# Attention row sums added up whole on two engines, and a side lane with pinned places

## The chip, the cores and the metric

The kernel runs on one core of a Trainium2 chip. The core has five instruction queues that run side by side and wait for each other through semaphores: PE (TensorE, the matrix engine; its weight loads are listed as PEld), DVE (VectorE), ACT (ScalarE), POOL (GpSimd) and SP (SyncE, which here only issues DMAs). Each queue runs its instructions strictly in the order in which the program lists them. The metric is the device time of one execution in microseconds (us), lower is better. Three runs of the kernel before gave 2798.85, 2803.77 and 2807.2 us.

## What is computed

One layer of a streaming encoder for two groups of requests: a prompt of 2048 frames and a sample group of 8 streams with 16 new frames each and 1024 cached ones. Cut to what matters here:

```python
u, q, k, v, logf = _mixer_inputs(x, ...)          # one projection, two groups of heads
# group A: depthwise conv of width 31, LayerNorm over 512 channels, swish
y32 = (y32 - mu) * lax.rsqrt(var + EPS) * ln_g + ln_b
# group B: attention, 8 heads of 64, causal, with a forget bias
s = einsum('bqhd,bkhd->bhqk', q, k) * HEAD_DIM ** -0.5
s = s + (cum_q[..., :, None] - cum_k[..., None, :])
p = softmax(where(mask, s, NEG_INF))
attn = einsum('bhqk,bkhd->bqhd', p, v)
x = x + g1 * (concat([conv_out, attn]) @ w_out)   # output projection
x = x + g2 * ((silu(h @ w_gate) * (h @ w_up)) @ w_down)
```

The softmax needs, for each query, the sum of the exponentials over all keys; it is computed with the keys on the 128 partitions, so a sum over keys is a sum over partitions and over key tiles.

## The kernel before

The program has these stages in time: input projections (to about 575 us), the prompt's attention (to about 1178 us), the output projection, and the feed-forward part (from about 1290 us to the end).

**Attention.** `attention` runs 16 *steps*, one for each pair of heads `p` (4) and block `qb` of 512 queries (4). A step goes over `4 * qb + 4` key tiles `kt` of 128 keys. For each key tile and each of the two heads, `attend` issues two matmuls into a bank `s` (L1004, L1010), a third with the mask on the diagonal (L1012), and one exponential on ACT into a tile `e` (L1014). Such a head and key tile is called a *unit* below; there are 320. Two key tiles later `values` multiplies `e` with V into `pv` (L971), both heads side by side in the array. Tiles with `kt < 4 * qb` lie below the diagonal and are 512 queries wide; the four others are 512, 384, 256 and 128 wide.

**Sums.** Below the diagonal POOL adds the exponentials of two neighbouring key tiles, for each head, into `two` (L980); PE multiplies each `two` with a matrix of ones into the bank `sm` (`add_up`, L960). Four such matmuls fit side by side in the array: a matmul with a group number `g` writes 32 rows of `sm` from row 32 g on. Diagonal tiles go into `sm` without an addition.

**Maxima.** `score_maxima` runs some 30 to 50 units ahead: it multiplies the same queries and keys once more (`mx`, L923, two banks) and DVE reduces each product to a maximum (`M`, L928). PE's second next `mx` waits for its bank, so for that reduction.

**End of a step.** ACT copies `pv` to `zc` (L991; `zc` has two buffers, so step n+2 takes that of step n) and `sm` to SBUF; the sums go through DRAM to another layout (`load`), are inverted on DVE (`invert`, L1058), come back spread over partitions (`back`), and DVE multiplies `zc` by them (`divide`, L1066), after which SP stores `zc` to `cat_d` (L1067). These four are due 2, 6, 9 and 14 units after the end of the step.

**The lane.** `background` is work with no place of its own in the attention: the conv's LayerNorm for five chunks (`conv_norm`), then the whole attention of the sample group (`sample_setup`, eight times `sample_batch`). It has one PSUM bank (`lane`), so each of its matmuls waits for the reader of the one before. A batch is a chain: keys times queries for two halves of the cache and the new frames (L1074), each added to `S` on DVE (L1175), maximum (L1181), exponential on ACT (L1182), transposes (L1189, L1195) with copies on ACT, probabilities times V (L1207), scaling (L1211), a transpose (L1214) and two copies into `catS` (L1217). Each `yield` in it is a point between which the weaving of the generators sets attention work.

**Order.** A list scheduler decides the order on each queue from priorities (the lane's are 1000 lower, `BACK_BY`) and its own estimate of when operands are there. `after` forbids an instruction to be set ahead of a named one on the same engine, without a wait. The wrapper `behind` did this for some of the lane's matmuls.

The output projection (`project_out`) takes all eight PSUM banks as accumulators `acc` (L1244), that of the lane for the last of the eight column blocks.

Of the kernel before, what the change touches and what calls it, by code (L numbers as in the profile page):

```python
# [118 lines left out]
class Layer:  # L119
# [587 lines left out]
    def conv_norm(self, ch, sp, bank):  # L707
# [9 lines left out]
        def channel_mean(src):  # L717
            pm = bank
            for j in range(4):
                self.behind(nc.tensor.matmul)(pm[32 * j:32 * j + 32, :n], self.ones[:, 0:32], src[j], start=True, stop=True,  # L720
                                 tile_position=(0, 32 * j))
            m = sp.tile([P, 512], F32, tag="cm", name="cm")
            nc.scalar.copy(m[:, :n], pm[:, :n])
            po = bank
            nc.tensor.matmul(po[:, :n], self.mean, m[:, :n], start=True, stop=True)
            return po

        mu = channel_mean([y[:, j, :n] for j in range(4)])
        ms = sp.tile([P, 512], F32, tag="cw", name="cmu")
        nc.scalar.copy(ms[:, :n], mu[:, :n])  # L730
        yield
        sqs = []
        for j in range(4):
            nc.vector.tensor_tensor(y[:, j, :n], y[:, j, :n], ms[:, :n], ALU.subtract)
            sq = sp.tile([P, 512], F32, tag="cq", name="cq", bufs=4)
            nc.scalar.activation(sq[:, :n], y[:, j, :n], AF.Square)
            sqs.append(sq[:, :n])
        yield
        var = channel_mean(sqs)
        v = sp.tile([P, 512], F32, tag="cv", name="cvar")[:, :n]  # L740
        nc.vector.tensor_scalar(v, var[:, :n], EPS, None, ALU.add)
        r = sp.tile([P, 512], F32, tag="cr", name="cr")[:, :n]
        nc.scalar.activation(r, v, AF.Ln)
        nc.scalar.activation(r, r, AF.Exp, scale=-0.5)
        newton_rsqrt(nc, r, sp.tile([P, 512], F32, tag="cm", name="ct")[:, :n], v, 1)
        yield
        for j in range(4):
            z = y[:, j, :n]
            nc.vector.tensor_tensor(z, z, r, ALU.mult)
# [30 lines left out]
    def attention(self, ctx):  # L780
# [4 lines left out]
        self.waiting, self.due, self.last_s = [], [], None  # L785
# [11 lines left out]
        nback, done, units, scored = 15 + 5 * 9 + 12 + 8 * 11, 0, 0, AHEAD  # L797
# [147 lines left out]
    def attend(self, p, qb, n):  # L945
# [5 lines left out]
        z, sums = [], []  # L951

        started = set()

        def add_up(terms, last=False):
            if terms and not started:
                z.append(self.bank("tr", "sm"))
# [7 lines left out]
        def values(kt, off, es):  # L965
# [10 lines left out]
            if kt < 4 * qb:  # L976
                if kt % 2 == 0:
                    for h in range(2):
                        two = wk.tile([P, 512], F32, tag="two", name="two", bufs=6)
                        nc.gpsimd.tensor_tensor(two, es[h], self.waiting[0][3][h], ALU.add)  # L980
                        sums.append((2 * (kt // 2 % 2) + h, 0, two))
                elif kt % 4 == 1:
                    ready, sums[:] = sums[:-2], sums[-2:]
                    add_up(ready)
                return
            sums.extend((2 * (kt % 2 if qb else 0) + h, off, es[h]) for h in range(2))
            if kt % 2 == 0:
                return
            if kt == nkt - 1:
                zc = wk.tile([P, 512], F32, tag="zc", name="zc")  # L990
                self.last_exp = nc.scalar.copy(zc, z[0])  # L991
            add_up(sums, kt == nkt - 1)
            sums.clear()
            if kt == nkt - 1:
                self.end_of_step(p, qb, zc, z[1])

        for kt in range(nkt):
# [4 lines left out]
            for h in range(2):  # L1002
# [10 lines left out]
                e = wk.tile([P, 512], F32, tag="e", name="e", bufs=12)  # L1013
# [17 lines left out]
    def end_of_step(self, p, qb, zc, sums):  # L1031
# [37 lines left out]
        self.due += [(self.nscore + k, f) for k, f in ((2, load), (6, invert), (9, back), (14, divide))]  # L1069

    def behind(self, op):

        def issue(*args, **kw):
            ins = op(*args, **kw)  # L1074
            self.after(ins, self.last_s)
            return ins
        return issue

    def sample_setup(self, bank):
# [27 lines left out]
        for kt in range(8):  # L1107
            self.behind(nc.tensor.matmul)(pt[:n, 2 * kt:2 * kt + 2], lf[:, kt, :], self.ones[:, 0:2], start=True, stop=True)
        suf = sm.tile([P, 8], F32, name="suf")
        nc.vector.memset(suf[:n, 7:8], 0.0)  # L1110
        for kt in range(6, -1, -1):
            nc.vector.tensor_tensor(suf[:n, kt:kt + 1], pt[:n, 2 * kt + 2:2 * kt + 3], suf[:n, kt + 1:kt + 2], ALU.add)
        yield
        for b in range(2):
            pb = bank.rearrange("p (i k) -> p i k", i=4)
            for i in range(4):
                self.behind(nc.tensor.matmul)(pb[:n, i, :], lf[:, 4 * b + i, :], tri, start=True, stop=True)
            nc.vector.tensor_tensor(
                bias[:n, b * 512:(b + 1) * 512].rearrange("p (i k) -> p i k", i=4), pb[:n],
# [7 lines left out]
        nc.tensor.matmul(pn[:n, :], lm.rearrange("p s h -> p (s h)"), sel[:, NS:], start=True, stop=True)  # L1127
# [25 lines left out]
    def sample_batch(self, b, bank):  # L1153
# [4 lines left out]
        for c in range(3):  # L1158
# [8 lines left out]
            pc = bank  # L1167
            for g in range(NP):
                self.behind(nc.tensor.matmul)(pc[32 * g:32 * g + 32, :w], self.Qbd[:, g, b].rearrange("p h q -> p (h q)"), kt[:, g, :],
                                              start=True, stop=True, tile_position=(0, 32 * g))  # L1170
# [4 lines left out]
            nc.vector.tensor_tensor(S[:, c0:c0 + w], S[:, c0:c0 + w], pc[:, :w], ALU.add)  # L1175
            if c == 2:
                nc.vector.tensor_tensor(S[:, c0:], S[:, c0:], self.maskS, ALU.add)
            yield
        nm = sm.tile([P, 1], F32, tag="nm", name="nm", bufs=2)
        rs = sm.tile([P, 1], F32, tag="rsx", name="rsx", bufs=2)  # L1180
        nc.vector.tensor_reduce(nm, S, AX.X, ALU.max, negate=True)  # L1181
        nc.scalar.activation(S, S, AF.Exp, bias=nm, accum_out=rs)  # L1182
        nc.vector.reciprocal(rs, rs)
# [582 lines left out]
```

## Time and profile before

| | before |
|---|---|
| median of 3 runs | 2803.77 us |
| the profiled execution | 2804.06 us, of which 2802.3 us are the span of its instructions |
| PE busy | 2719.9 us, 97% |
| DVE busy | 1975.1 us, 70% |
| ACT busy | 1237.1 us, 44% |
| POOL busy | 461.2 us, 16% |
| mean granted TensorE clock | 0.985 |

Busy shares are of the whole span. PE is a pipeline whose ends are modelled, so a busy PE can still wait a little inside a matmul. In a row of the groups, "x96 | 127.2, 1342 | 398.3 <-ACT e" reads: 96 instructions, 127.2 us busy (overlaps counted once), 1342 ns for one, and 398.3 us in which the engine sat idle before them, mostly for that ACT instruction. A row of the timeline begins with its start and length in us; an idle time ahead of it, if any, stands in brackets at its end with what ended it. An fp32 matmul counts as two instructions there.

### The profile page before, as it was taken

To read this page: it belongs to the slowest core of one execution; us is meant where nothing else is said; L and a number is where in the kernel's file an instruction comes from. 1 tells how busy PE (TensorE), PEld (TensorE's weight loads), DVE (VectorE), ACT (ScalarE), POOL (GpSimd) and SP (SyncE) were. 2 spreads that over 40 slices of the span, in tenths; PEclk is the share of its full clock that TensorE was granted. 3 is DMA by queue.
4 is the path that set the end of the run, shared out by engine and by line. 5 is a ranking of instruction groups with operands and counts; after the bars stand their busy time and mean duration, and the time that the engine had idled before them with its cause. 6 is when DMAs were issued, how large, how long until landed. Compare 5 with 4: busy or idle time off the path is not lost. (4 is left out here: it accounts for less than half of the span.)

```text
span 2802.3 us, 48143 instructions
## 1 busy us (share of the span) xinstructions
PE 2719.9 (97%) x16666; PEld 2388.6 (85%) x16666; DVE 1975.1 (70%) x3951; ACT 1237.1 (44%) x2406; POOL 461.2 (16%) x616
## 2 busy tenths in 40 slices
PE   7999999999999999999999999999999999999999
PEld 6899988864445545499999999999999999999999
DVE  2798898966465454235397989877886778766765
ACT  4443323344343444434354446444554446555552
POOL 3454411222222222214201121000000000000000
PEclk9999999989999999999999999999999999999999
DMA  9753567674426676355576869866786769788873
GB/s 328 248 192 107 189 220 265 203 199 123 124 73 192 175 233 176 116 192 187 177 265 205 305 204 314 272 217 214 240 288 208 227 194 319 245 279 262 274 252 116
DMA packets 406348, 603.49 MB, mean 215 GB/s; under 512 B 61556, under 2 KB 264468, under 8 KB 404056
## 3 DMA queue, kind: packets, MB, share of 16 engines
q1 hardware_dynamic: 405976, 600.31, 66.7%
q8 instruction: 131, 2.15, 0.3%
q14 instruction: 113, 0.93, 0.1%
q0 software_dynamic: 128, 0.11, 0.0%
HBM read 426.00 MB, written 174.25 MB: 214 GB/s over the span
## 5 line engine op out<-in xcount | busy, mean ns | idle before, releaser
L1556 PE MATMUL z<-rT,rW 128*128 128x360 f32 (+1 forms) x8316 | 1383.7, 328 | 4.5 <-ACT rW L1260 1.4
L1556 PEld LDWEIGHTS z<-rT,rW 128*128 128x128 f32 x8316 | 1379.8, 188 | 6.3 <-ACT rW L1260 2.1
L1260 ACT ACTIVATE rW<-rR 128x512 fp32r<-128x512 f32 x714 | 434.1, 616 | 382.5 <-PE z L1556 275.9
L1261 DVE TENSOR_TENSOR rW<-rR,rW 128x512 fp32r<-128x512 f32 x714 | 476.8, 673 | 149.3 <-ACT rW L1260 144.7
L702 DVE SCALAR_TENSOR_TENSOR cv<-cu,cpar,cv 128x384 f32<-128x384 f32 x580 | 311.7, 615 | 2.9 <-ACT cv L700 2.9
L928 DVE TENSOR_REDUCE M<-mx 128x1 f32<-128x512 f32 (+2 forms) x320 | 189.7, 607 | 146.5 <-PE mx L923 105.2
L1014 ACT ACTIVATE e<-s 128x512 f32<-128x512 f32 (+3 forms) x320 | 168.4, 533 | 278.2 <-PE s L1012 140.2
L514 PE MATMUL z<-hqx,wqh 128*128 128x384 f32 (+1 forms) x768 | 197.5, 333 | 0.1
L980 POOL TENSOR_TENSOR two<-e 128x512 f32<-128x512 f32 x96 | 127.2, 1342 | 398.3 <-ACT e L1014 328.0
L1260 ACT ACTIVATE rT<-traw 128x360 fp32r<-128x360 f32 (+1 forms) x315 | 149.3, 501 | 91.7 <-DMA traw<-gt_d 58.1
L1261 DVE TENSOR_TENSOR rT<-traw,rT 128x360 fp32r<-128x360 f32 (+1 forms) x315 | 157.7, 531 | 42.7 <-ACT rT L1260 42.4
L923 PEld LDWEIGHTS mx<-K,Q 96*128 96x128 f32 x320 | 63.7, 201 | 116.6 <-DVE M L928 54.7
L923 PE MATMUL mx<-K,Q 96*128 96x512 f32 (+2 forms) x320 | 145.2, 463 | 17.1 <-DVE M L928 12.6
L971 PE MATMUL pv<-e,V 128*64 128x512 f32 (+3 forms) x640 | 156.6, 565 | 3.0 <-ACT zc L991 3.0
L514 PEld LDWEIGHTS z<-hqx,wqh 128*128 128x128 f32 x768 | 136.0, 188 | 16.6 <-issue 12.4
L1484 DVE TENSOR_TENSOR rR<-rR 128x512 f32<-128x512 f32 (+1 forms) x136 | 94.2, 712 | 57.2 <-DMA rR<-w_down 52.0
L1244 PE MATMUL acc<-ch,woh 128*128 128x360 f32 (+1 forms) x384 | 128.1, 336 | 4.9 <-DVE xo L1252 2.6
L1244 PE MATMUL acc<-ch,wol 128*128 128x360 f32 (+1 forms) x384 | 128.1, 334 | 0.0
L1004 PE MATMUL s<-Q,K 128*128 128x512 f32 (+3 forms) x320 | 127.6, 399 | 0.0
L514 PE MATMUL z<-hqx,wql 128*128 128x384 f32 (+1 forms) x384 | 126.5, 329 | 0.0
L1244 PE MATMUL acc<-cl,woh 128*128 128x360 f32 (+1 forms) x384 | 122.3, 331 | 0.0
L1010 PE MATMUL s<-Q,K 128*128 128x512 f32 (+3 forms) x320 | 119.3, 373 | 0.0
(307 smaller groups left out, 3581.5 us busy)
## 6 DMA issues: line engine op xcount, KB each, us to landing
rR<-sup_d SPq DMA_DIRECT2D x176, 256.0 KB
rR<-w_gate SPq DMA_DIRECT2D x132, 256.0 KB
traw<-gt_d SPq DMA_DIRECT2D x154, 180.0 KB
rR<-w_down SPq DMA_DIRECT2D x104, 256.0 KB
rR<-sdn_d SPq DMA_DIRECT2D x96, 256.0 KB
rR<-w_up SPq DMA_DIRECT2D x88, 256.0 KB
sup_d<-rR SPq DMA_DIRECT2D x88, 256.0 KB
wa<-w_ada SPq DMA_DIRECT2D x16, 1024.0 KB
```

The costliest lines, as they stand in the source:

```text
L514: nc.tensor.matmul(z[:, :n], w[:, m], x[:, :n], start=(c == 0 and k == 0), stop=(c == CB - 1 and k == 2))
L702: self.pin(nc.vector.scalar_tensor_tensor(dst, src, w, acc[i], ALU.mult, ALU.add))
L923: self.mx.append(nc.tensor.matmul(mx[:, :w], Q2[0:AUX, h, j * P:(j + 1) * P], K2[kb][0:AUX, h, :w], start=True, stop=not diag))
L928: self.last_max = nc.vector.tensor_reduce(M[:, i, kb:kb + 1], mx[:, :w], AX.X, ALU.max)
L971: product = nc.tensor.matmul(z[0][HD * h:HD * h + HD, off:], V[kt // 4][:, kt % 4, HD * h:HD * h + HD], es[h][:, off:], start=(kt == 0), s ...
L980: nc.gpsimd.tensor_tensor(two, es[h], self.waiting[0][3][h], ALU.add)
L1004: first = nc.tensor.matmul(s[:, off:], K1[kb][:, h, sl], Q1[:, h, off:], start=True, stop=False)
L1014: self.last_piece = nc.scalar.activation(e[:, off:], s[:, off:], AF.Exp)
L1244: self.nc.tensor.matmul(z[:, :n], w[:, m], y, start=(first and i == 0 and k == 0), stop=(last and i == len(terms) - 1 and k == 2))
L1260: copy = self.nc.scalar.activation(hi, raw, AF.Copy)
L1261: engine.tensor_tensor(lo, raw, f32(hi), ALU.subtract)
L1556: nc.tensor.matmul(z, W[:, x, m], t[:, y, :w], start=(k == 0 and i == 0), stop=(k == n - 1 and i == 2))
```

## The change

It has five parts.

1. Below the diagonal the exponentials of a whole step are added up, key tile by key tile, into one tile for each head: head 0's on POOL, head 1's on DVE. PE multiplies the two with the ones once for each step. The groups of the diagonal tiles change so that the first diagonal tile goes beside the two sums; the three others follow at the step's end. `two` goes, `sums` (4 buffers) comes, and `e` has 14 buffers for 12.
2. In `conv_norm` the subtraction of the mean and the product with the reciprocal deviation, each for four tiles, go from DVE to POOL.
3. All lane operations on PE, ACT, DVE and POOL are issued through one wrapper `late`, which keeps each behind the latest attention instruction of its own engine (last `s`, last exponential, last maximum, last addition). The first DVE additions of `attend` use it too.
4. The lane has more yields; the count by which they are spread over the attention is 237 in place of 160.
5. The four pieces of work at a step's end are due 3, 8, 13 and 20 units after it, in place of 2, 6, 9 and 14.

```diff
         def channel_mean(src):
-            pm = bank
             for j in range(4):
-                self.behind(nc.tensor.matmul)(pm[32 * j:32 * j + 32, :n], self.ones[:, 0:32], src[j], start=True, stop=True,
-                                 tile_position=(0, 32 * j))
+                self.pe(bank[32 * j:32 * j + 32, :n], self.ones[:, 0:32], src[j], start=True, stop=True, tile_position=(0, 32 * j))
+            yield
             m = sp.tile([P, 512], F32, tag="cm", name="cm")
-            nc.scalar.copy(m[:, :n], pm[:, :n])
+            self.copy(m[:, :n], bank[:, :n])
+            yield
...
         for j in range(4):
-            nc.vector.tensor_tensor(y[:, j, :n], y[:, j, :n], ms[:, :n], ALU.subtract)
+            self.gp(y[:, j, :n], y[:, j, :n], ms[:, :n], ALU.subtract)
+        yield
+        for j in range(4):
             sq = sp.tile([P, 512], F32, tag="cq", name="cq", bufs=4)
-            nc.scalar.activation(sq[:, :n], y[:, j, :n], AF.Square)
+            self.act(sq[:, :n], y[:, j, :n], AF.Square)
             sqs.append(sq[:, :n])
-        yield
+            yield
...
         for j in range(4):
             z = y[:, j, :n]
-            nc.vector.tensor_tensor(z, z, r, ALU.mult)
+            self.gp(z, z, r, ALU.mult)
...
-        nback, done, units, scored = 15 + 5 * 9 + 12 + 8 * 11, 0, 0, AHEAD
+        nback, done, units, scored = 232 + 5, 0, 0, AHEAD
...
             self.last_product = product
-            if kt < 4 * qb:
-                if kt % 2 == 0:
-                    for h in range(2):
-                        two = wk.tile([P, 512], F32, tag="two", name="two", bufs=6)
-                        nc.gpsimd.tensor_tensor(two, es[h], self.waiting[0][3][h], ALU.add)
-                        sums.append((2 * (kt // 2 % 2) + h, 0, two))
-                elif kt % 4 == 1:
-                    ready, sums[:] = sums[:-2], sums[-2:]
-                    add_up(ready)
+            d = kt - 4 * qb
+            if d < 0:
+                if kt == 0:
+                    held.extend(es)
+                elif kt == 1:
+                    acc.extend(wk.tile([P, 512], F32, tag="acc", name="sums", bufs=4) for h in range(2))
+                if kt:
+                    self.last_add = nc.gpsimd.tensor_tensor(acc[0], es[0], acc[0] if kt > 1 else held[0], ALU.add)
+                    self.late(nc.vector.tensor_tensor, self.last_max)(acc[1], es[1], acc[1] if kt > 1 else held[1], ALU.add)
                 return
-            sums.extend((2 * (kt % 2 if qb else 0) + h, off, es[h]) for h in range(2))
-            if kt % 2 == 0:
-                return
-            if kt == nkt - 1:
+            if d == 0:
+                held[:] = [(h, 0, x) for h, x in enumerate(acc)]
+            part = 2 * (d % 3 == 0 if qb else 0)
+            held.extend((part + h, off, es[h]) for h in range(2))
+            if d == 3:
                 zc = wk.tile([P, 512], F32, tag="zc", name="zc")
                 self.last_exp = nc.scalar.copy(zc, z[0])
-            add_up(sums, kt == nkt - 1)
-            sums.clear()
-            if kt == nkt - 1:
+                add_up(held, True)
                 self.end_of_step(p, qb, zc, z[1])
+            elif d == 1:
+                n = 4 if qb else 2
+                add_up(held[:n])
+                del held[:n]
...
-                e = wk.tile([P, 512], F32, tag="e", name="e", bufs=12)
+                e = wk.tile([P, 512], F32, tag="e", name="e", bufs=14)
...
-        self.due += [(self.nscore + k, f) for k, f in ((2, load), (6, invert), (9, back), (14, divide))]
+        self.due += [(self.nscore + k, f) for k, f in ((3, load), (8, invert), (13, back), (20, divide))]
-    def behind(self, op):
+    def late(self, op, last):
 
         def issue(*args, **kw):
             ins = op(*args, **kw)
-            self.after(ins, self.last_s)
+            self.after(ins, last)
             return ins
         return issue
+    def pe(self, *args, **kw):
+        return self.late(self.nc.tensor.matmul, self.last_s)(*args, **kw)
+    def gp(self, *args):
+        return self.late(self.nc.gpsimd.tensor_tensor, self.last_add)(*args)
```

`flip` (transposes), `act`, `copy` and `dve` are wrappers of the same kind. In `sample_setup` and `sample_batch` every operation with a partner on another engine goes through them, with a yield ahead of most of those that wait.

The scheduler decides the order on each queue anew. Three places.

**PE, from the last attention matmul to the output projection.** `R` is the last one, with which the last step's sums are spread; `lane<-kc` are the key products of a sample batch, `lane<-ident,S` its transposes, `lane<-vc` and `lane<-vn` its products with V, `lane<-ident,ob` its last transpose. Before, the lane rows from `R` on, up to the first matmul `acc`, and then those that follow, the first of them behind 14 `acc`, the others behind 63:

```order
L1043 MATMUL R<-sm,four 128x512
L1074 MATMUL lane<-kc,Qbd 32x512 x4
L1074 MATMUL lane<-kS,Qbd 32x16 x4
L1189 MATMUL lane<-ident,S 128x128 x4
```

```order
L1189 MATMUL lane<-ident,S 128x128 x4
L1195 MATMUL lane<-ident,S 16x128
L1207 MATMUL lane<-vc,pT 32x128 x32
L1207 MATMUL lane<-vn,pTn 32x128 x4
L1214 MATMUL lane<-ident,ob 128x128
```

That is one batch, the eighth, and its first key products already stand ahead of `R`. In the changed kernel the rows around `R`, and then those behind the 63 matmuls `acc`, are these (L1086 is the line of the wrapper `late`):

```order
L1055 MATMUL R<-sm,four 128x512
L1086 MATMUL lane<-ident,ob 128x128
L1086 MATMUL lane<-kc,Qbd 32x512 x8
L1086 MATMUL lane<-kS,Qbd 32x16 x4
```

```order
L1086 MATMUL lane<-ident,S 128x128 x8
L1086 MATMUL lane<-ident,S 16x128
L1086 MATMUL lane<-vc,pT 32x128 x32
L1086 MATMUL lane<-vn,pTn 32x128 x4
L1086 MATMUL lane<-ident,ob 128x128
L1086 MATMUL lane<-kc,Qbd 32x512 x8
L1086 MATMUL lane<-kS,Qbd 32x16 x4
L1086 MATMUL lane<-ident,S 128x128 x8
L1086 MATMUL lane<-ident,S 16x128
L1086 MATMUL lane<-vc,pT 32x128 x32
L1086 MATMUL lane<-vn,pTn 32x128 x4
L1086 MATMUL lane<-ident,ob 128x128
```

The fence ends with the seventh batch; the eighth follows in the same rows, with nothing between, and then the other `acc`. The last transpose of the fifth batch, the sixth, the seventh and the eighth batch now stand behind the last attention matmul. Counted by the units ahead of them on PE, the lane starts its first batch at unit 195 in place of 156 of 320, and the conv's LayerNorm ends at 170 in place of 135.

**DVE, around the division of step (1, 3).** `M` are the maxima, `zc` the division. Before:

```order
L928 TENSOR_REDUCE M_1_6655<-mx_10280 128x1
L1066 TENSOR_TENSOR zc_10030<-zc_10030,aR_10038 128x512
L1058 RECIPROCAL inv_10204<-inv_10204 128x8
L928 TENSOR_REDUCE M_1_6655<-mx_10309 128x1
```

and now:

```order
L938 TENSOR_REDUCE M_1_6655<-mx_9981 128x1
L1078 TENSOR_TENSOR zc_9612<-zc_9612,aR_9622 128x512
L1070 RECIPROCAL inv_9780<-inv_9780 128x8
L1086 TENSOR_TENSOR bias_9242<-lane_7504,suf_9323 64x512
L938 TENSOR_REDUCE M_1_6655<-mx_10022 128x1
```

The division moved from unit 182 to unit 187 (by the maxima ahead of it), and that of steps (0, 3) and (2, 3) alike, from 103 to 107 and from 262 to 267. ACT's copy into the same buffer two steps later, for steps (1, 1), (2, 1) and (3, 1), stands behind 108, 188 and 268 exponentials before, and behind 110, 190 and 270 now. SP's store of `zc` stands between the two in both.

**DVE, in a step below the diagonal,** here (2, 3). `sums` is the new addition for head 1:

```order
L938 TENSOR_REDUCE M_0_6654<-mx_10774 128x1
L1086 RECIPROCAL rsx_9858<-rsx_9858 128x1
L938 TENSOR_REDUCE M_0_6654<-mx_10789 128x1
L1086 TENSOR_TENSOR sums_10639<-e_10724,sums_10639 128x512
L938 TENSOR_REDUCE M_0_6654<-mx_10803 128x1
L938 TENSOR_REDUCE M_0_6654<-mx_10813 128x1
L1086 TENSOR_TENSOR sums_10639<-e_10768,sums_10639 128x512
```

There are 84 such additions on DVE and 84 for head 0 on POOL, in place of 96 on POOL; the matmuls with the ones below the diagonal fall from 96 to 24.

More of the change, by code (lines that the diff above doesn't have):

```diff
@@ L717, in channel_mean @@
         def channel_mean(src):
-            pm = bank
             for j in range(4):
-                self.behind(nc.tensor.matmul)(pm[32 * j:32 * j + 32, :n], self.ones[:, 0:32], src[j], start=True, stop=True,
-                                 tile_position=(0, 32 * j))
+                self.pe(bank[32 * j:32 * j + 32, :n], self.ones[:, 0:32], src[j], start=True, stop=True, tile_position=(0, 32 * j))
+            yield
             m = sp.tile([P, 512], F32, tag="cm", name="cm")
-            nc.scalar.copy(m[:, :n], pm[:, :n])
[L724 to L728, printed above, removed]
+            self.copy(m[:, :n], bank[:, :n])
+            yield
+            self.pe(bank[:, :n], self.mean, m[:, :n], start=True, stop=True)
+            yield
+        yield from channel_mean([y[:, j, :n] for j in range(4)])
         ms = sp.tile([P, 512], F32, tag="cw", name="cmu")
-        nc.scalar.copy(ms[:, :n], mu[:, :n])
+        self.copy(ms[:, :n], bank[:, :n])
         yield
@@ L950, in attend @@
         nkt = 4 * qb + 4
-        z, sums = [], []
-        started = set()
+        z, held, acc, started = [], [], [], set()
         def add_up(terms, last=False):
-            if terms and not started:
+            if not started:
                 z.append(self.bank("tr", "sm"))
@@ L1107, in sample_setup @@
         for kt in range(8):
-            self.behind(nc.tensor.matmul)(pt[:n, 2 * kt:2 * kt + 2], lf[:, kt, :], self.ones[:, 0:2], start=True, stop=True)
+            self.pe(pt[:n, 2 * kt:2 * kt + 2], lf[:, kt, :], self.ones[:, 0:2], start=True, stop=True)
+        yield
         suf = sm.tile([P, 8], F32, name="suf")
@@ L1188, in sample_batch @@
             for i in range(4):
-                nc.tensor.transpose(pp[:, i, :], S[:, (4 * c + i) * P:(4 * c + i + 1) * P], self.ident)
+                self.flip(pp[:, i, :], S[:, (4 * c + i) * P:(4 * c + i + 1) * P], self.ident)
+            yield
             pT = sm.tile([P, 4, P], F32, tag="pT", name="pT", bufs=2)
-            nc.scalar.copy(pT, pp)
+            self.copy(pT, pp)
             pts.append(pT)
-            yield
+        yield
         pp = bank[:, :P]
-        nc.tensor.transpose(pp[:QS, :], S[:, PAST:], self.ident)
+        self.flip(pp[:QS, :], S[:, PAST:], self.ident)
+        yield
         pn = sm.tile([P, P], F32, tag="pTn", name="pTn")
-        nc.scalar.copy(pn[:QS, :], pp[:QS, :])
-        vn = sm.tile([QS, DC], F32, tag="vn", name="vn")
-        nc.sync.dma_start(vn, a["o_v"][T + b * QS:T + (b + 1) * QS, :])
+        self.copy(pn[:QS, :], pp[:QS, :])
         yield
```

72 lines of the change are left out of this document (46 added, 26 removed).

## Prediction

> **What bounds the kernel now.** I read the page's first part, then the busy time by stretches, then the groups and waits of the attention, the only stage whose code changes.
>
> ```profile
> span 2802.3 us, 48143 instructions
> PE 2719.9 (97%) x16666; PEld 2388.6 (85%) x16666; DVE 1975.1 (70%) x3951; ACT 1237.1 (44%) x2406; POOL 461.2 (16%) x616
> 630.00:1177.00 547.00, 526.32 (x3122) 262.50 (x3123) 271.88 (x501) 224.18 (x438) 131.77 (x102) 0.98 0.52 152
> 1177.00:1205.00 28.00, 19.23 (x169) 15.60 (x163) 14.71 (x22) 15.20 (x24) 0.00 (x0) 0.88 0.41 132
> ```
>
> The last two rows are stretches: length, then busy time and count of PE, PEld, DVE, ACT and POOL, then granted clock, DMA share and GB/s. PE is busy for 526 of 547 us of attention, VectorE for half of it. So PE's queue sets the stage: whatever takes PE time or makes PE wait counts in full, and work that moves between other engines counts only where PE waits for it. The second row is the seam to the output projection, where PE is busy for 19 of 28 us, at a clock of 0.88. All later stages keep their code and their PE work, so a delay at the seam reaches the end undiminished. I sum against the profiled execution, 2804.06 us (span 2802.3 and 1.76 around it); the median of the runs, 2803.77, is 0.3 lower, which I neglect.
>
> **1. Fewer matmuls for the sums: -14 us.**
>
> ```profile
> 630.00:1178.00 548.00, 59.10 (x448) 12.53 (x448) 0.98 0.51 151
> L960 PE MATMUL sm<-two,ones 128*32 128x512 f32 x192 | 26.4, 624 | 0.0
> 1172.62 1.06 PE L960 MATMUL sm<-two,ones 128*32 128x512 f32 x8
> 1173.50 1.03 PE L960 MATMUL sm<-e,ones 128*32 128x512 f32 x8
> 1174.46 0.65 PE L971 MATMUL pv<-e,V 128*64 128x256 f32 x4
> ```
>
> The first row is the stretch with line 960 alone: 59 us of PE for all sums. The 192 instructions on `two` are 96 matmuls at 26.4 / 96 = 0.275 us; 72 go, 19.8 us. The starts of the last three rows show that a batch of four side by side takes 0.88 to 0.96 us. But the diagonal tiles of 384 and 256 columns now use the same rows of `sm` one after the other, where the first of them ran beside a wider tile: some 0.45 us more in each of 12 steps, 5.4. Net -14. PE is the bound here, so all of it is on the path; ends -10 and -20.
>
> **2. Two sample batches leave the attention: -13 us.**
>
> ```profile
> 890.00:1177.00 287.00, 53.81 (x758) 27.24 (x760) 17.62 (x45) 9.93 (x21) 0.99 0.63 188
> ```
>
> This is the lane's tile alone: 53.8 us of PE for seven batches and a part of the setup, at most 7.7 each, and 6.5 without the setup and the pipeline's ends. By the order two whole batches, and little more, move from there to the seam: -13 (ends -10, -16).
>
> **3. The seam: +36 us.** The changed PE queue holds batches six, seven and eight behind `R`, and from the sixth's transposes on nothing else. Their chain has to be paid one instruction at a time:
>
> ```profile
> 1017.24 1.04 PE L1074 MATMUL lane<-kc,Qbd 128*32 128x512 f32 x8
> 1018.35 0.69 DVE L1175 TENSOR_TENSOR S<-S,lane 128x512 f32<-128x512 f32 x1 [2.33 <-PE lane L1074]
> 1182.86 0.26 PE L1074 MATMUL lane<-kS,Qbd 128*32 128x16 f32 x8 [3.00 <-DVE S L1175]
> 1186.30 1.11 PE L1189 MATMUL lane<-ident,S 128*128 128x128 f32 x4 [3.19 <-ACT S L1182]
> 1187.18 0.68 PE L1244 MATMUL acc<-ch,woh 128*128 128x368 f32 x1
> 1190.90 0.60 PE L1189 MATMUL lane<-ident,S 128*128 128x128 f32 x4
> 1199.58 0.27 PE L1195 MATMUL lane<-ident,S 128*16 128x128 f32 x1
> 1201.24 1.96 PE L1207 MATMUL lane<-vc,pT 128*32 128x128 f32 x64 [1.40 <-ACT pTn L1197]
> 1203.68 0.35 DVE L1211 TENSOR_SCALAR ob<-lane,rsx 128x128 f32<-128x128 f32 x1 [1.90 <-PE lane L1207]
> 1204.45 0.46 DVE L1217 COPY catS<-lane 64x64 f32<-64x64 f32 x2 [0.42 <-PE lane L1214]
> L1191 ACT COPY pT<-lane 128x512 f32<-128x512 f32 x16 | 9.4, 585 | 6.5 <-PE lane L1189 6.5
> ```
>
> Key products to the end of their addition take 1018.35 + 0.69 - 1017.24 = 1.80, with a hand-over 1.9, twice 3.8. From the new frames' products to the first transposes (addition, mask, maximum, exponential) 1186.30 - 1182.86 = 3.4. Transposes 0.60 and a copy 0.59 with two hand-overs 1.3, twice 2.6; the third, small, 0.7. Products with V 1203.68 - 1201.24 = 2.4; the rest to the end of the copies 1204.91 - 1203.68 = 1.2. Together 14 us a batch, in which PE works 6.5. Before, PE spent 1204.9 - 1199.6 = 5.3 us here behind the 63 `acc`, to which the row at 1199.58, the third transpose, is next. Now it spends the second half of batch six, 2.6 + 0.7 + 2.4 + 1.2 = 7, and twice 14: 35, which is 29.7 more. Ahead of the 63 `acc` come two key products more, about 2 us, and the loads of `cat_d` queue on SP behind a load of new keys that waits for the sixth batch's first product, 1 to 3. So +33 at full clock. But PE is idle for more than half of it:
>
> ```profile
> 1183.00:1190.00 7.00, 3.81 (x21) 3.55 (x17) 3.59 (x8) 3.50 (x7) 0.00 (x0) 0.51 0.75 233
> ```
>
> With PE busy for 3.81 of 7 us the granted clock was 0.51. At half clock a batch's two large key products grow by about 0.9 each and its products with V by 1, some 3 us; I take half of that for two batches: +36 (ends +29, +42). The Trainium skill's page "TensorE: Matmul & The Clock Gate", section "Why this matters for your kernels", advises against idle gaps of about 3 us between bursts of matmuls, after which the array is back at half rate; by that rule all of both batches would run slow, and the term would be +39. The row above agrees.
>
> **4. LayerNorm off VectorE: -12 us.**
>
> ```profile
> 708.90 4.64 DVE L734 TENSOR_TENSOR cy<-cy,cmu 128x512 f32<-128x512 f32 x4
> 709.41 2.99 POOL L980 TENSOR_TENSOR two<-e 128x512 f32<-128x512 f32 x2 [18.64 <-ACT e L1014]
> 714.07 0.50 PE L923 MATMUL mx<-K,Q 96*128 96x512 f32 x1 [1.89 <-DVE M L928]
> 690.30 0.39 PE L923 MATMUL mx<-K,Q 96*128 96x256 f32 x1 [1.62 <-DVE M L928]
> 797.53 0.79 PE L923 MATMUL mx<-K,Q 96*128 96x512 f32 x1 [3.16 <-DVE M L928]
> PE mx L923 <- DVE M L928: 9.5, 8, 3.2
> PEld mx L923 <- DVE M L928: 46.6, 50, 4.0
> ```
>
> Four such operations in a row hold VectorE for 4.6 us; the maxima stand behind them, and PE's `mx` behind those. PE's pure idle time of that kind is 9.5 us in 8 pieces, the three rows 6.7 of it; the weight loads' 46.6 are mostly covered by a matmul still running. The operations now run on POOL, free for three quarters of the stage. I take the 9.5 and a few us of half clock after the larger gaps: -12 (ends -5, -20).
>
> **5. Additions on VectorE: +10 us.** The trace has no such addition. The nearest rows:
>
> ```profile
> L1066 DVE TENSOR_TENSOR zc<-zc,aR 128x512 f32<-128x512 f32 x15 | 10.3, 685 | 16.6 <-DMA aR<-inv_d 16.5
> L734 DVE TENSOR_TENSOR cy<-cy,cmu 128x512 f32<-128x512 f32 x16 | 16.4, 1089 | 0.0
> L980 POOL TENSOR_TENSOR two<-e 128x512 f32<-128x512 f32 x96 | 127.2, 1342 | 398.3 <-ACT e L1014 328.0 <-PE sm L960 70.3
> L928 DVE TENSOR_REDUCE M<-mx 128x1 f32<-128x512 f32 x224 | 151.9, 687 | 112.6 <-PE mx L923 105.2 <-PE mx L927 6.0
> 1012.68 1.08 PE L971 MATMUL pv<-e,V 128*64 128x512 f32 x4
> 1015.35 1.08 PE L971 MATMUL pv<-e,V 128*64 128x512 f32 x4
> 1023.90 1.08 PE L971 MATMUL pv<-e,V 128*64 128x512 f32 x4
> 1026.51 1.08 PE L971 MATMUL pv<-e,V 128*64 128x512 f32 x4
> ```
>
> The same shape took 0.685 us where POOL was idle and 1.09 in the mean where it mostly ran beside additions of POOL (in the rows at 708.90, 1.16). POOL now adds head 0's tile as VectorE adds head 1's, so I take 1.0: 84 us. On average VectorE stays at 272 - 34 + 84 - 11 = 311 of some 520 us. But in a key tile below the diagonal it has two maxima (1.37), an addition (1.0) and about 0.3 of other work, 2.7, while PE takes 2.7 and 2.6 between the first two and the last two rows, products of V one key tile apart, where it is densest, and 547 / 160 = 3.4 on average. A late maximum then costs PE a little: 0.12 us in each of 84, 10 us (ends 0 and 34, the latter below). The other queue that waits is ACT, for `e` buffers, but it has seven key tiles of room.
>
> **6. A later division: +9 us.**
>
> ```profile
> ACT zc L991 <- DMA cat_d<-zc: 7.4, 2, 4.5
> 1097.29 0.58 ACT L991 COPY zc<-pv 128x512 f32<-128x512 f32 x1 [4.51 <-DMA cat_d<-zc]
> 1097.93 1.98 PE L971 MATMUL pv<-e,V 128*64 128x512 f32 x4 [2.99 <-ACT zc L991]
> ```
>
> Already before, ACT waits twice for the store that frees a `zc` buffer, 7.4 us together, and PE lost 2.99 by the longer wait. The order brings division and copy from 6 units apart to 3, at about 1.4 us a unit 4 us closer, at steps (1, 1), (2, 1) and (3, 1). Behind the copy wait ACT's exponentials, and behind these the three `s` banks. So three waits grow by up to 4: +9 (ends 0, +15). What the later dates relieve, the 16.5 us in which VectorE waited for `aR`, is in term 7.
>
> **7. Pins, yields and the rest: -3 us.** More room between a lane instruction and its partner spares PE some waits, as for `aR`; bounds -10 and +8, as nothing in the trace prices it. What POOL gained and the exponentials' longer stay are hidden under PE.
>
> Sum: -14 - 13 + 36 - 12 + 10 + 9 - 3 = +13, so 2804 + 13 = **2817 us**.
>
> **The rivals.** (a) *The terms cancel.* VectorE keeps up and the stores land in time, terms 5 and 6 are 0: 2804 - 14 - 13 + 36 - 12 - 3 = 2798. For it: VectorE is busy only half the stage. Against: stores waited already. (b) *Faster: VectorE's maxima never hold PE any more.* Of the 46.6 us behind M much was real loss; then the attention gains 40 rather than 12 on term 4, with 5 and 6 at 0: 2804 - 14 - 13 + 36 - 40 - 3 = 2770. It decides from the point where each maximum ends within one key tile's PE time, 2.6 us. Against: the 9.5 us of pure idling. (c) *The port makes VectorE the bound.* If each addition waits for a whole one of POOL's, it takes POOL's 1.34 us; a key tile then needs 1.37 + 1.34 + 0.3 = 3.0 on VectorE against 2.6 in PE's densest tiles: 84 x 0.4 = 34 rather than 10: 2841. The rows at 708.90 speak for a part of it, 1.16 rather than 1.34. The Trainium skill's page "SBUF — State Buffer", section "Who interferes with whom", says that a VectorE instruction with two SBUF inputs and a GpSimd instruction that reads SBUF exclude each other for the whole instruction; by that rule (c) holds wherever the two meet. The group means above, 685 against 1089 ns, agree that they do.
>
> **How the numbers follow.** Forecast 0.42 (its own range 2808 to 2828), (a) 0.27, (b) 0.16, (c) 0.15. A measurement tells 0.3% from no change, 8.4 us. Faster by more: (b) and a quarter of (a), 0.2. Slower by more: (c) and most of the forecast, 0.5. Within: 0.3. The range reaches from between (b) and (a) to (c): 2786 to 2842.
>
> **What would show it.** Right: the attention's last matmul some 20 to 35 us earlier than 1178; behind the first `acc` some 35 us in which PE runs lane rows only, at a clock near 0.5; POOL busy for about 150 us in the attention; `sums` on VectorE near 1.0 us; ACT's waits for `cat_d<-zc` three and longer. Wrong: a seam under 25 us (then term 3), an attention that ends before 1140 (then 4 to 6), or `mx` idle of PE over 30 us (then (c)).

## The result, and the profile after

The changed kernel takes 2821.14 us (median of 4 runs, 2818.5 to 2823.88); the kernel before, run beside it, 2802.4 us. The ratio is 1.0066 (95% interval 1.0046 to 1.0085), so the change costs 18.5 us. The prediction was 2817. The profiled execution took 2823.88 us, with this span and these busy times on the first lines of its page:

```profile
span 2822.1 us, 48016 instructions
PE 2725.8 (97%) x16522; PEld 2385.6 (85%) x16522; DVE 2009.7 (71%) x3995; ACT 1241.8 (44%) x2408; POOL 488.0 (17%) x644
```

PE is still the bound. Its timeline around the last attention matmul `R` tells where the time lies, first that of before, then that of the changed kernel:

```profile
1177.74 1.13 PE L1043 MATMUL R<-sm,four 128*128 128x512 f32 x2
...
1205.05 0.41 PE L1244 MATMUL acc<-ch,woh 128*128 128x368 f32 x1 [0.64 <-DVE catS L1217]
```

```profile
1149.98 1.12 PE L1055 MATMUL R<-sm,four 128*128 128x512 f32 x2 [0.37 <-ACT sm L1050]
...
1162.94 0.67 PE L1279 MATMUL acc<-ch,woh 128*128 128x368 f32 x1 [2.83 <-ACT ch L1295]
...
1176.40 0.60 PE L1086 MATMUL lane<-ident,S 128*128 128x128 f32 x4
...
1187.34 1.06 PE L1086 MATMUL lane<-kc,Qbd 128*32 128x512 f32 x8 [0.55 <-DVE catS L1086]
...
1198.83 3.64 PE L1086 MATMUL lane<-vc,pT 128*32 128x128 f32 x64 [0.34 <-ACT pTn L1086]
...
1204.46 1.07 PE L1086 MATMUL lane<-kc,Qbd 128*32 128x512 f32 x8 [0.55 <-DVE catS L1086]
...
1222.14 0.41 PE L1279 MATMUL acc<-ch,woh 128*128 128x368 f32 x1 [0.64 <-DVE catS L1086]
```

`R` comes 27.8 us earlier (1177.74 - 1149.98). But from `R` to the `acc` that goes on behind the lane it now takes 72.2 us, before 27.3: 44.8 lost at the seam. From there to the end of the span it is 1600.0 and before 1597.3. So -27.8 + 44.8 + 2.7 = 19.8 us, the difference of the spans. By stretches (length, busy time and count of PE, PEld, DVE, ACT and POOL, granted clock, DMA share, GB/s) the seam of the changed kernel is:

```profile
1150.00:1163.00 13.00, 4.92 (x28) 1.04 (x28) 7.42 (x11) 1.82 (x3) 0.00 (x0) 0.71 0.66 236
1163.00:1176.40 13.40, 13.40 (x63) 13.38 (x64) 5.00 (x9) 8.96 (x14) 0.00 (x0) 0.77 0.75 255
1176.40:1222.00 45.60, 26.18 (x296) 15.02 (x293) 10.71 (x24) 10.08 (x18) 0.00 (x0) 0.66 0.46 159
```

The last row is the serial block that was forecast: 45.6 us behind the 63 `acc` with nothing but lane rows on PE, at a granted clock of 0.66. No engine is busy for much more than half of it; each waits for the next. The clock was not low throughout. In the seventh batch it was 1.00 during the key products, and 0.50 from the first transposes, which begin behind a wait of 3.06 us:

```profile
1187.34:1191.40 4.06, 2.39 (x24) 0.47 (x24) 1.38 (x2) 0.00 (x0) 0.00 (x0) 1.00 1.02 338
1194.40:1198.80 4.40, 2.61 (x9) 1.52 (x9) 0.15 (x1) 1.43 (x3) 0.00 (x0) 0.50 0.89 328
```

The attention's groups (instructions | busy time, mean ns | idle time before them) and waits (total, times, longest) of the changed kernel answer to those shown of before:

```profile
L992 POOL TENSOR_TENSOR sums<-e,sums 128x512 f32<-128x512 f32 x72 | 95.3, 1324 | 108.1 <-ACT e L1026 100.6 <-DMA sum_d<-sm 5.6 <-ACT pTn L1086 1.4
L1086 DVE TENSOR_TENSOR sums<-e,sums 128x512 f32<-128x512 f32 x72 | 62.4, 867 | 3.3 <-ACT e L1026 2.7
L1086 POOL TENSOR_TENSOR cy<-cy,cmu 128x512 f32<-128x512 f32 x16 | 21.7, 1388 | 13.4 <-ACT cmu L1086 13.4
L1078 DVE TENSOR_TENSOR zc<-zc,aR 128x512 f32<-128x512 f32 x15 | 13.2, 877 | 2.2 <-DMA aR<-inv_d 2.2
```

```profile
PEld mx L933 <- DVE M L938: 45.8, 64, 1.8
PE mx L933 <- DVE M L938: 8.0, 14, 1.4
ACT zc L1001 <- DMA cat_d<-zc: 4.6, 2, 3.5
```

The new addition on VectorE takes 867 ns, between the two neighbouring rows from before. PE's pure waits of `mx` for maxima are 8.0 us, before 9.5, but now in small pieces: the longest is 1.4 us, before 3.2. ACT's waits for `cat_d` did not grow.

### The profile page after: what moved, and what is told of

Its sections match the earlier page's. It is cut to its first block, busy times and chain, and to the rows that moved or that the text cites. A ratio compares the mean times of both kernels' runs of the same rounds, so it can differ in the third digit from the quotient of the medians.

```text
span 2822.1 us, 48016 instructions
## 1 busy us (share of the span) xinstructions
PE 2725.8 (97%) x16522; PEld 2385.6 (85%) x16522; DVE 2009.7 (71%) x3995; ACT 1241.8 (44%) x2408; POOL 488.0 (17%) x644
## 4 chain that ended last, share of the span: by engine, by line
PE 82%; DMA 7%; DVE 6%; issue 2%; ACT 2%; POOL 1%; SPq 1%; DVEq 0%; ACTq 0%; POOLq 0%
PE z L1591 45%; PE z L514 5%; PE acc L1279 5%; PE pv L980 4%; PE lane L1086 3%; PE pa L322 3%; PE pvv L342 3%; PE pg L322 3%; PE mx L933 3%; PE s L1016 2%; PE s L1022 2%; PE sm L969 2%; DMA wraw<-w_in 1%; DVE ca L702 1%; DVE M L938 1%
## 5 line engine op out<-in xcount | busy, mean ns | idle before, releaser
L1279 PE MATMUL acc<-ch,woh 128*128 128x360 f32 (+1 forms) x384 | 127.6, 335 | 10.9 <-ACT ch L1295 5.4
L992 POOL TENSOR_TENSOR sums<-e,sums 128x512 f32<-128x512 f32 x72 | 95.3, 1324 | 108.1 <-ACT e L1026 100.6
```

Source lines behind the costliest of these rows:

```text
L1279: self.nc.tensor.matmul(z[:, :n], w[:, m], y, start=(first and i == 0 and k == 0), stop=(last and i == len(terms) - 1 and k == 2))
```

## The experiments

Each kernel is compared with the kernel before, run beside it, as a ratio of times; "us" is (ratio - 1) x 2802. Two stretches are read from the timeline of the one profiled execution: the attention, from the first `s` to `R`, and from `R` to the end of the span. That execution can lie some 6 us from the median of its kernel (e9's is its fastest, e10's its slowest). An interval of a ratio is some 0.001 to 0.002 to each side, so a difference of two rows is sure to 4 to 7 us.

| kernel | ratio (95% interval) | us | attention | `R` to end |
|---|---|---|---|---|
| before | 1 | 0 | 556.3 | 1624.6 |
| changed | 1.0066 (1.0046, 1.0085) | +18.5 | 530.2 | 1672.1 |
| e1: changed, lane's priority 50 | 0.9973 (0.9962, 0.9984) | -7.6 | 549.9 | 1622.2 |
| e2: changed, old dates | 1.0092 (1.0079, 1.0105) | +25.8 | 533.2 | 1672.8 |
| e3: changed, all additions on POOL | 1.0034 (1.0022, 1.0046) | +9.5 | 514.8 | 1673.1 |
| e4: before, new sums | 1.0063 (1.0050, 1.0076) | +17.7 | 576.1 | 1622.7 |
| e5: before, norm on POOL | 0.9919 (0.9905, 0.9932) | -22.7 | 527.5 | 1622.0 |
| e6: e1, norm on VectorE | 0.9993 (0.9982, 1.0004) | -2.0 | 549.2 | 1621.1 |
| e7: e1, all additions on POOL | 0.9907 (0.9893, 0.9920) | -26.1 | 519.3 | 1631.9 |
| e8: before, new sums, all additions on POOL | 0.9975 (0.9966, 0.9985) | -7.0 | 550.3 | 1620.9 |
| e9: e1, old sums, norm on VectorE | 0.9909 (0.9894, 0.9924) | -25.5 | 529.2 | 1615.6 |
| e10: e1, old sums | 0.9918 (0.9904, 0.9932) | -23.0 | 530.2 | 1624.6 |
| e11: before, new sums, norm on POOL | 0.9980 (0.9971, 0.9990) | -5.6 | 546.8 | 1628.1 |
| e12: before, norm and all additions on POOL | 0.9926 (0.9910, 0.9941) | -20.7 | 523.5 | 1632.1 |

### e1: the lane inside the attention

```diff
-MAXIMA_BY, BACK_BY = 30, 1000
+MAXIMA_BY, BACK_BY = 30, 50
```

> The changed kernel, with the lane's priority 50 below the attention's instead of 1000 (BACK_BY 50). In the order that follows, the eighth batch's key products stand behind units 309 and 312 of 320, so no whole batch is left behind the last attention matmul R. Theory (the seam is the loss): from R to the first acc behind the 63, 72.2 us become 25 to 30, as before the change (27.3); three batches return into the attention at 6.5 to 7 us of PE each, so it ends 18 to 22 us later than 1150. Time 2821 - 45 + 20 = 2796, 2790 to 2802. Rival (the attention is short only because the batches left it, a batch costs there what it costs alone, about 15 us): attention's end 45 later, time 2818 to 2824.

2792.61 us. PE's timeline of this run around `R`:

```profile
1166.75 1.12 PE L1055 MATMUL R<-sm,four 128*128 128x512 f32 x2
...
1172.39 0.33 PE L1086 MATMUL lane<-ident,ob 128*128 128x128 f32 x1 [0.81 <-DVE ob L1086]
1177.99 0.68 PE L1279 MATMUL acc<-ch,woh 128*128 128x368 f32 x1 [5.27 <-ACT ch L1295]
```

The lane's last transpose is at 1172.39, ahead of the first `acc`. From `R` to the end it takes 1622.2 instead of 1672.1, and the attention is 19.7 us longer. So a batch costs some 7 us of PE inside the attention and 17 at the seam. The seam was the loss, and the rival (a batch costs there what it costs alone) falls.

### e2: the dates

```diff
-        self.due += [(self.nscore + k, f) for k, f in ((3, load), (8, invert), (13, back), (20, divide))]
+        self.due += [(self.nscore + k, f) for k, f in ((2, load), (6, invert), (9, back), (14, divide))]
```

> The changed kernel with the old due times 2, 6, 9, 14. The lane's key products stay at the same units. Theory (term 6 of the prediction: the later division makes ACT wait for cat_d at three places): 9 us less, 2812, and ACT's waits of zc for cat_d, 4.6 us in two, shrink. Rival (those waits were no longer than before the change, 7.4 us in two, so the dates cost nothing): 2818 to 2824, and VectorE waits again some 10 us or more for aR.

2824.46 us: not faster, and by the ratios 7 us slower, which is hardly more than the noise. ACT's wait for `cat_d` is gone, but VectorE waits for `aR` again, 10.1 us in three instead of 2.2 in one:

```profile
DVE zc L1078 <- DMA aR<-inv_d: 10.1, 3, 7.6
```

The theory fell, and the rival held, down to the 10 us of waits for `aR`: the later dates cost nothing, and may gain a little.

### e3: all additions on GpSimd

```diff
-                    self.late(nc.vector.tensor_tensor, self.last_max)(acc[1], es[1], acc[1] if kt > 1 else held[1], ALU.add)
+                    self.last_add = nc.gpsimd.tensor_tensor(acc[1], es[1], acc[1] if kt > 1 else held[1], ALU.add)
```

> The changed kernel with both heads' additions on GpSimd, 168 of them, none on VectorE. The lane keeps its place (8th batch and the two before it behind R). Theory (term 5: additions on VectorE delay maxima and cost PE 10 us): 2811. Rival 1 (VectorE has the room, the additions are hidden): 2818 to 2824. Rival 2 (GpSimd at two additions a key tile, 2 x 1.3 = 2.6 us, against PE's 2.6 to 3.4, becomes the bound, exponential tiles are held longer and ACT waits for e): 2830 or more.

2807.53 us, 9 us less by the ratios and 13.6 by the medians; the attention is 15.4 us shorter. So the additions on VectorE cost about the 10 forecast by the ratios, and more by the attention. One part was in no expectation. In the changed kernel PE's timeline at a step's first diagonal tile reads

```profile
755.95 1.05 PE L969 MATMUL sm<-sums,ones 128*32 128x512 f32 x2
756.92 0.73 PE L933 MATMUL mx<-K,Q 96*128 96x512 f32 x2
...
758.81 0.62 PE L969 MATMUL sm<-sums,ones 128*32 128x512 f32 x1
758.81 0.62 PE L969 MATMUL sm<-e,ones 128*32 128x512 f32 x2
```

and in e3

```profile
822.74 0.62 PE L969 MATMUL sm<-sums,ones 128*32 128x512 f32 x2
822.75 0.62 PE L969 MATMUL sm<-e,ones 128*32 128x512 f32 x2
```

In the first, head 0's sum goes through PE alone for 0.97 us (756.92 - 755.95), then comes other work, then head 1's sum with the diagonal tiles. In e3 the two sums stand together and share one pass with the diagonal tiles. Presumably the scheduler takes head 1's sum, which VectorE makes behind its maxima, to be ready later. In the order of the changed kernel the two are apart in 10 of 12 steps, by 5 to 12 rows; in e3 by at most 3, and only two of the 12 steps have a pass for one sum alone. That is 10 us of PE. The stretch from 610 to 1200 us with the line of the sums alone shows it, for before, changed and e3:

```profile
610.00:1200.00 590.00, 59.10 (x448) 12.53 (x448) 0.96 0.52 152
```

```profile
610.00:1200.00 590.00, 51.26 (x304) 11.35 (x304) 0.96 0.50 148
```

```profile
610.00:1200.00 590.00, 41.31 (x304) 10.53 (x304) 0.95 0.49 151
```

PE saved 59.1 - 51.3 = 7.8 us on the sums, against 17.8 without VectorE in them. The other part shows at the maxima: the time from each `mx` to the next instruction on PE, added up over the attention, is 100.7 us in the changed kernel and 91.7 in e3. That late maxima make it is likely but not shown, since PE's pure waits of `mx` for maxima are the same in both, 8.0 and 8.1 us.

### e4 and e8: the new sums alone

Both put the changed `add_up` and `values` and 14 `e` buffers into the kernel before; e8 has the addition of head 1 as in e3.

```diff
+                    self.last_add = nc.gpsimd.tensor_tensor(acc[0], es[0], acc[0] if kt > 1 else held[0], ALU.add)
+                    self.behind2(nc.vector.tensor_tensor, self.last_max)(acc[1], es[1], acc[1] if kt > 1 else held[1], ALU.add)
```

> The kernel before with only the row sums changed (and 14 e buffers): 84 additions on POOL, 84 on VectorE, 24 sm matmuls on full sums below the diagonal. LayerNorm, pins, yields and dates are as before. By its order the eighth batch's first key products stand at units 305 and 308, ahead of where they were (320), so the seam behind R shrinks by 3 to 8. Theory (terms 1 and 5, -14 and +10, and the seam): 2804 - 4 - 5 = 2795. Rival 1 (the additions cost nothing): 2785. Rival 2 (port contention makes VectorE the bound, +34): 2819.

> The kernel before with only the row sums changed, and all 168 additions on GpSimd, none on VectorE. The eighth batch's key products stand at units 311 and 314. Theory (the additions on VectorE cost what e4 lost; without them only term 1, -14, and a seam shorter by 3 to 8 are left): 2801 - 14 - 5 = 2782, 2776 to 2790. Rival 1 (e4's loss is of the sums themselves, a sum that is ready late at each step's end): 2810 to 2818. Rival 2 (GpSimd holds exponential tiles too long): over 2800.

e4: 2817.48 us, 17.7 slower, near rival 2 in its number, though an addition on VectorE took only 0.77 us in the mean there. e8: 2789.80, 7.0 faster, at the slow end of what was expected. The additions on VectorE make 25 us between the two. So even where GpSimd adds everything, less than the 14 us of term 1 is left. The trace of e8 shows where much of it went: PE's waits for maxima grew to 17.6 us, from 9.7 in the kernel before. The three longest of them, 3.5 to 5.4 us, stand behind the LayerNorm's product on VectorE, which took up to 6.3 us for its four operations while GpSimd ran additions. One of the three, and the sum of all waits:

```profile
819.52 6.17 DVE L749 TENSOR_TENSOR cy<-cy,cr 128x512 f32<-128x512 f32 x4
826.35 0.79 PE L923 MATMUL mx<-K,Q 96*128 96x512 f32 x1 [5.45 <-DVE M L928]
PE mx L923 <- DVE M L928: 17.6, 9, 5.4
```

### e5: LayerNorm alone

```diff
-            nc.vector.tensor_tensor(y[:, j, :n], y[:, j, :n], ms[:, :n], ALU.subtract)
+            nc.gpsimd.tensor_tensor(y[:, j, :n], y[:, j, :n], ms[:, :n], ALU.subtract)
...
-            nc.vector.tensor_tensor(z, z, r, ALU.mult)
+            nc.gpsimd.tensor_tensor(z, z, r, ALU.mult)
```

> The kernel before with only the LayerNorm's subtraction and product on GpSimd. By its order the eighth batch stands a little later than before (its first key products just ahead of R and behind it). Theory (term 4: 12 us of PE's waits for maxima go): 2801 - 12 and up to 3 back at the seam, 2789 to 2793. Rival 1 (VectorE had room, and the three waits only move): 2799 to 2804. Rival 2 (rival b of the prediction, VectorE's maxima no longer hold PE): 2765 to 2775.

2774.82 us: 22.7 faster than the kernel before beside it (2797.14). The time lies at the upper end of rival 2; the gain lies between the theory's 8 to 12 and rival 2's 26 to 36, which were counted from 2801. In the stretch in which most of the LayerNorm lies, first before, then e5:

```profile
700.00:820.00 120.00, 111.78 (x521) 52.30 (x520) 66.55 (x104) 49.14 (x94) 26.17 (x18) 0.94 0.39 114
```

```profile
700.00:820.00 120.00, 118.36 (x601) 58.96 (x603) 58.98 (x102) 57.30 (x108) 54.74 (x44) 1.00 0.40 123
```

PE's idle time falls from 8.2 to 1.6 us, and the granted clock rises from 0.94 to 1.00, which by an estimate is worth up to 0.06 x 120 = 7 us more. The prediction had counted the waits and only "a few us" of clock. Of the waits for maxima 5.3 us are left in e5:

```profile
PE mx L923 <- DVE M L928: 5.3, 6, 2.2
```

### e6, e9, e10, e11: the parts beside each other

e6 and e9 take the LayerNorm back to VectorE (`self.gp` becomes `self.dve("tensor_tensor", ...)`). e9 and e10 take the old sums back, with 12 `e` buffers. e11 is e4 with the edit of e5.

```diff
-            self.gp(z, z, r, ALU.mult)
+            self.dve("tensor_tensor", z, z, r, ALU.mult)
```

> The changed kernel with the lane's priority 50, as in e1, and the LayerNorm's subtraction and product back on VectorE; the eighth batch's key products stand at units 309 and 312 as in e1. Theory (with additions on VectorE its four operations in a row hold the maxima longer; that is what made the sums alone, e4, 18 us slower than before): 15 to 25 above e1, 2808 to 2818. Rival (it was the pins and yields that took the 26 us between e4's attention and e1's): 2790 to 2797.

> The changed kernel, lane's priority 50, with the old sums (96 additions on POOL, 12 e buffers) and the LayerNorm back on VectorE: what is left of the change are the pins, the yields and the dates. The eighth batch's key products stand at units 313 and 316. Theory (term 7 and the dates are worth next to nothing, -3): 2790 to 2797 against 2797 before. Rival (the pins and yields give the 27 us by which e6's attention is shorter than e4's): 2768 to 2776.

> The changed kernel, lane's priority 50, with the old sums alone; LayerNorm on GpSimd, pins, yields and dates as changed. Its difference from e1 (2793) is what the new sums are worth in the changed kernel. Theory (terms 1 and 5 together, -14 + 10, are off by the cost of the additions: e3 and e7 gained 14 to 21 without them on VectorE, so the new sums cost 0 to 8): 2785 to 2793. Rival 1 (they cost what e4 lost alone, 18): 2772 to 2778. Rival 2 (they gain, as predicted): 2796 or more.

> The kernel before with the new sums and the LayerNorm on GpSimd; no pins, yields and dates. Additive (e4 +18, e5 -22 against 2797): 2789 to 2797, as e1, so pins, yields and dates are worth nothing there. Rival (pins, yields and dates are worth some 20 beside the additions on VectorE, which they keep behind the maxima): 2810 to 2818. The eighth batch's key products stand at units 319 and 320, just ahead of R.

e6 2792.39, e9 2770.44, e10 2772.67, e11 2791.32 us. With e1, e4, e5 and the kernel before these are all eight combinations, "new pins" meaning pins, yields, dates and the priority of 50 together:

| us against before | old sums | new sums | the sums cost |
|---|---|---|---|
| norm on VectorE, old pins | 0 | +17.7 (e4) | 17.7 |
| norm on POOL, old pins | -22.7 (e5) | -5.6 (e11) | 17.1 |
| norm on VectorE, new pins | -25.5 (e9) | -2.0 (e6) | 23.5 |
| norm on POOL, new pins | -23.0 (e10) | -7.6 (e1) | 15.4 |

Two things can be read. The new sums cost 15 to 24 us in each row, whatever stands beside them. And the LayerNorm on POOL and the new pins each take 23 to 26 us off alone, but no more together: they remove the same loss. e6's theory fell (once the pins are there, the LayerNorm on VectorE costs some 6 us beside the new sums, hardly more than the noise, and nothing beside the old ones), e9's too (its rival held), and of e10 rival 1 held. e11 came out as its additive case said, although its reason (that pins are worth nothing there) is only true where the LayerNorm is on POOL already.

In e9 the four LayerNorm operations still follow each other on VectorE, and PE waits for maxima less than in the kernel before (9.5 us):

```profile
731.18 4.66 DVE L1084 TENSOR_TENSOR cy<-cy,cmu 128x512 f32<-128x512 f32 x4
```

```profile
PE mx L933 <- DVE M L938: 6.7, 8, 3.3
```

So the burst itself was not all of the loss. The whole attention tells more, from 620 us to `R`, for before, e5 and e9:

```profile
620.00:1177.74 557.74, 536.80 (x3159) 269.71 (x3158) 277.66 (x512) 228.34 (x448) 133.22 (x104) 0.97 0.51 151
620.00:1147.20 527.20, 516.81 (x3155) 261.80 (x3154) 246.72 (x469) 229.43 (x448) 173.65 (x144) 0.99 0.52 160
620.00:1148.40 528.40, 518.25 (x3175) 261.51 (x3173) 274.32 (x515) 230.59 (x450) 130.50 (x104) 0.99 0.52 159
```

PE's idle time falls by half in both, from 20.9 to 10.4 and 10.2 us, and the granted clock rises alike. The waits for maxima (9.7, then 5.3 and 6.7 us) are less than half of what goes. By an estimate from these rows, 0.02 of 558 us, the clock is worth 11 us; the rest of the shorter busy time, 7 to 9 us, has no cause shown here. Which of pins, yields, dates and the priority of 50 takes it off was not separated; the kernel before with the priority alone was not run.

### e7 and e12: towards a faster kernel

e7 is e1 with the edit of e3, e12 is e8 with the edit of e5.

> The changed kernel with the lane's priority 50 and both heads' additions on GpSimd. Theory (the two gains add: 28 us of e1, 14 of e3; but the eighth batch stands behind R again, as in the kernel before, which costs the seam up to 12): 2779 to 2790. Rival (both took away the same loss): 2793 or more.

> The kernel before with the LayerNorm on GpSimd and the new sums with all additions on GpSimd; no pins, yields and dates. The eighth batch stands behind R. If the two gains add (e5 -22, e8 -7): 2764 to 2770, better than e5 (2775) and e7 (2772). Rival (GpSimd, now with 168 additions and 40 operations of the LayerNorm, holds exponential tiles too long, or both took the same loss): 2772 or more.

e7: 2771.71 us, better than both and below the theory's range: its gain is some 9 us more than those of e1 and e3 added up. No run says why. e12: 2775.64, where the gains do not add, as its rival said. In both the eighth batch stands behind `R` again: 1632 us from `R` to the end against 1616 to 1625 in e5, e9 and e10, so a part of what their attention gained is given back there. e9, e7, e10 and e5 cannot be told from each other; all beat both kernels by 0.8 to 0.9% (before) and about 1.5% (changed).

## Why the prediction came out right

The total, +13 against +18.5 measured, was right for the reason it named, the seam. Among the other terms two errors of some 17 and 19 us met with opposite signs, and that they cancelled to 2 us is luck: with either alone the forecast would have been off by 17 us or more.

- **Terms 2 and 3, the displaced lane: -13 + 36 = +23.** Right. e1 puts the lane back, and the time falls by 26.1 us (18.5 + 7.6). The seam itself was +44.8 rather than +36. Ahead of the 63 `acc` it grew by 3.5 us (12.96 from `R` to the first `acc`, 9.4 before), as forecast. Behind them a batch took 17.1 us (1204.46 - 1187.34) and the next 17.7, where 14 and half of 3 were taken. The prediction took half of 3 us for the slow clock, and a batch paid all of it, but not where it was sought. The products with V took 3.64 us instead of 1.96, the forecast being 1 us more, and the transposes 1.1 instead of 0.6; the large key products, which were to grow by 0.9 each, took 1.06 and 1.07 us in the seventh batch, as in the attention, and only one of the eighth's was slow (1.67). By the rule of the Trainium skill's page "TensorE: Matmul & The Clock Gate", section "Why this matters for your kernels", the term would have been +39; the measured size is nearer to that than to the half that was taken, but that all of a batch would run slow, as the prediction read the rule, the trace does not show. And 10.9 us passed for the rest of the sixth batch (1187.34 - 1176.40), where 7 were taken. In the attention the difference to e1 is 19.7 us for nearly three batches, where 13 were taken for two and little more.
- **Terms 1 and 5, the new sums: -14 + 10 = -4.** The step that failed. They cost 15 to 24 us. Term 1 assumed that 72 matmuls leave at the price of a full pass of four. But in 10 of 12 steps one of the two sums now takes a pass alone, which the order showed and the prediction did not look at: -7.8 rather than -14. Term 5 (+10) was too small: the same additions on POOL made e8 25 us faster than e4, e7 18.5 faster than e1, and e3 9 faster than the changed kernel, and some 10 of that are the passes. An addition took 867 ns, less than the 1.0 us assumed, so it was not its length that was mis-sized but what each costs PE. Rival (c), +34 by additions of 1.34 us, had the sign of this and not the mechanism: half of the additions took 0.68 us or less.
- **Term 4, the LayerNorm: -12.** Too small: -22.7 alone (e5). The wait that it named was there, but only 4.4 us of the 9.7 went; the rest came from other idle time of PE, from the clock, and in part from what no run explains. Rival (b) had the size better, not the reason. Beside the pins it is worth nothing that can be measured with the old sums (e10 against e9) and some 6 us with the new (e1 against e6).
- **Term 6, the dates: +9.** Wrong. ACT's waits for `cat_d` were 4.6 us in two, not three longer ones. They do come with the later dates, as with the old ones none is left (e2). But the path from them to PE failed: the changed kernel has no wait of PE for `zc`, where the kernel before had one of 2.99 us.
- **Term 7, the pins: -3.** Far too small alone: -25.5 in e9, priority and dates included, though it is the same loss as that of term 4.

By the runs the sum is -23.0 (pins, dates and LayerNorm, with the lane inside, e10), +15.4 (the sums, e1 against e10) and +26.1 (the lane displaced, the changed kernel against e1): +18.5. The prediction's sum has -6 for the first (terms 4, 6 and 7), -4 for the second and +23 for the third.

## What to carry to other kernels

Work of low priority that a list scheduler fills into an engine's gaps is cheap only as long as there are gaps: a batch cost 7 us inside the attention and 17 behind it, so after a change look first at what stands behind the last instruction of the stage it hid in. Matmuls that pay only because they run side by side must be ready side by side: two halves of one sum made on two engines were placed apart and each took a pass. And when two parts of a change aim at the same wait, try each alone: here either took off 23 us and both together no more.

## What the runs showed of the hardware

A VectorE operation with two SBUF inputs took longer when it met an operation of GpSimd, although it does the same. The product `zc`, with its shortest, median and longest time in ns, in the kernel before, the changed one and e3:

```profile
L1066 DVE TENSOR_TENSOR zc<-zc,aR x15: 673/682/693, 678.5 to 1148.6; 128x512 f32<-128x512 f32 x15
L1078 DVE TENSOR_TENSOR zc<-zc,aR x15: 679/685/1772, 690.0 to 1127.8; 128x512 f32<-128x512 f32 x15
L1078 DVE TENSOR_TENSOR zc<-zc,aR x15: 681/693/4378, 678.6 to 1111.2; 128x512 f32<-128x512 f32 x15
```

The mean grows from 685 to 877 and 1293 ns, but the median hardly moves. In the changed kernel four of all 16 products took over 0.75 us, and just these four began while an addition of GpSimd was running. So it is not GpSimd's load that sets the mean but how often the two meet: in e8 GpSimd is busy for 227 us of the attention and the mean is 808 ns, in e5 for 174 us and it is 999. A wait can outlast several of GpSimd's operations when they follow each other without a gap. In e3 a product of only 8 columns, which took 152 ns at best, ended with the fifth addition in a row, and PE's next `mx` sat idle for 4.37 us behind it:

```profile
718.95 5.76 DVE L1069 TENSOR_TENSOR inv<-inv 128x8 f32<-128x8 f32 x1
```

The maxima of 512 columns, which read PSUM, took 687 to 688 ns in before, changed and e3. That such operations of the two engines meet at a price was forecast, from the Trainium skill's page "SBUF — State Buffer", section "Who interferes with whom", and the rows agree.

The clock was a price of its own. In 700 to 820 us of the kernel before PE was idle for 8.2 of 120 us, in pieces of 3.2 us at most, and the granted clock was 0.94; with 1.6 us idle it was 1.00.
